# Differential attention: first block's weights split straight from its bank in all units, row sums at a unit's end, add and store in the next unit

## The chip, the core and the metric

The kernel runs on one core of a Trainium2 chip. The time is that of one execution on the device in microseconds (us). Five engines work side by side, each through its own instructions in order: PE (TensorE, matmuls and transposes; its weight loads are listed as PEld), DVE (VectorE), ACT (ScalarE), POOL (GpSimd) and SP (SyncE, which here issues the transfers). They meet only through semaphores.

## The reference

Two layers work on 1024 latent tokens and 256 context tokens of width 1024. Layer 0 has differential attention, layer 1 a state-space mixer; an MLP follows each. Only the attention of layer 0 matters here. For each of 8 heads there are two score maps, and their difference weights the values:

```python
s = jnp.einsum('bqhcd,bkhcd->bhcqk', q, k).astype(jnp.float32)
p = jax.nn.softmax(s, axis=-1)
w = p[:, :, 0] - lam * p[:, :, 1]
o = jnp.einsum('bhqk,bkhe->bqhe', w.astype(v.dtype), v)
return rmsnorm(o, subln_g) * (1.0 - lambda_init)
```

Queries and keys are rotated before (`apply_rope`), with a swap of the two halves of each head's coordinates.

## The kernel before

Everything is float32. A matmul operand is split into a high part (a copy rounded to fp32r) and a low part (the rest), and each product is three matmuls, `mm3` (lines 132 to 134): high by high, high by low, low by high.

The attention, `phase_b`, goes through 8 heads of 9 units; this text calls them head 0 to 7 and unit 0 to 8. Unit 0 takes the 256 context queries against 256 context keys, units 1 to 8 take 128 latent queries each against all 1280 keys. The order of the instructions on PE, DVE, ACT and POOL is the order in which the loop over `n` writes them (`manual_schedule`), so an instruction that waits holds up all that is written behind it on its engine.

A unit's own work is a chain: PE computes the scores (L579). DVE takes the row maximum and copies the scores out, once for each of the two maps (L592; in unit 0 L588). ACT exponentiates each (L602; in unit 0 L599), called exp 0 and exp 1 here. DVE combines the two maps into the weights: a reciprocal, a small product (L610, L611), and the long L613 over 1280 columns. In the next unit PE transposes these weights in three parts of 4, 2 and 4 tiles (L625; L620 where the unit before was unit 0), part 0, 1 and 2. Each part is split into halves in `wT` in one of two ways:

- `w_direct`: ACT copies the high half straight from PSUM (L631), DVE subtracts to get the low half (L632, it reads PSUM too);
- `w_copy`: ACT copies the part from PSUM to SBUF (L638), and POOL makes both halves from the copy (L641, L642). POOL cannot read PSUM.

One unit later, for a pair of units, PE multiplies the values (`values`, 30 `mm3` matmuls of 256 columns), ACT copies the output (L732), POOL squares it (L733), and PE sums the squares over the partitions (`pair_sums`: two L739 matmuls of one column, which write columns 0 and 1 of bank 6, then ACT's L740).

The PE also computes the next head's keys and queries in pieces called fills (`proj_group`, 8 products of three matmuls, in bank 7), in units 0, 1, 2, 3, 5 and 7; `FILLS` says how many products stand in each of the three places of a unit. In units 0, 3, 5 and 7 such a group then needs four steps: `evac` at the unit's end (ACT L528, DVE L529, and four transfers that swap halves), and three more that wait in the list `post`: `sine` (POOL L534, which waits for the swap), `add` (DVE L537), `store` (the split, ACT L137 and DVE L138). In units 1 and 2 the group has no rotation and is split at once (`direct`: L523, L524). In head 7 the fills are the output projection instead, with one product left for the last place of units 3, 5 and 7, and `out` (L855).

There are two kinds of unit. Units 4, 6 and 8 of heads 0 to 6 (`inside`) have no fills; PE does scores, half of the values, part 0 (in bank 7), the rest of the values, parts 1 and 2. Unit 1, and in head 7 units 4, 6 and 8 as well, stand in the same branch (line 946) but with fills. Units 0, 2, 3, 5 and 7 stand in the other branch (line 978): scores, part 0, a fill, parts 2 and 1, a fill. L772 (DVE) scales the outputs of the head before, in units 7, 8, 0, 1 and 2.

`next_post` runs one step of `post`. Before, the first branch calls it twice, the second once, so that `sine` and `add` come in the unit after the group and `store` in the one after that.

Of the kernel before, what the change touches and what calls it, by code (L numbers as in the profile page):

```python
# [70 lines left out]
class Prog:  # L71
# [610 lines left out]
    def phase_b(self):  # L682
# [38 lines left out]
        def values(h, pair, k0=0, k1=10):  # L721
            V = loaded[h, "v"]
            last = 2 if pair == 0 else 10
            for kt in range(k0, min(k1, last)):
                self.mm3(pb[:, 0:256], V[0][:, kt], V[1][:, kt], self.wT[0][:, kt], self.wT[1][:, kt],
                         kt == 0, kt == last - 1)
# [42 lines left out]
        def norm_pair(h, pair):  # L769
            i = nloaded.pop(0)  # L770
            (nob, nrb), (nhi, nlo) = nbufs[i], nsplit[i]
            nc.vector.scalar_tensor_tensor(nob, nob, self.sg, nrb, ALU.mult, ALU.mult)  # L772

            def halves():
                self.split(nhi, nlo, nob, nc.gpsimd)
                for j, t in enumerate((nhi, nlo)):
                    self.dma(self.on[h, j, :, 256 * pair : 256 * pair + 256], t.bitcast(F32))

            return halves
# [91 lines left out]
        def next_post():  # L871
            f = post.pop(0) if post else None
            if f:
                f()

        with self.manual():
            for n in range(72 + 5):
# [32 lines left out]
                inside = late and not groups  # L910
                low, high, last, whole = pb[:, 0:512], pb[:, 256:512], self.bank(7), self.PS[:, 1280:1792]

                def fill(i):
                    for f in fills[i]:
                        f()

                def part(i, tb):
                    return self.w_part(prev[1], prev[2], i, tb) if i < parts else None

                def direct(w):  # L920
                    if w:
                        self.w_direct(*w)

                def copied(*ws):
                    for f in [self.w_copy(*w) for w in ws if w]:
                        f()

                def exps(c):
                    if front:
                        self.exps(u, c, p, sm, s0, sn)  # L930

                def output(*a):
                    pair_out(*a)
                    sums.append((n + (parts != 1), lambda: pair_sums(*a)))
                    if a[0] == 7:
                        tail.append((n + 1, a[1]))

                def do_sums():
                    while sums and sums[0][0] <= n:
                        sums.pop(0)[1]()  # L940

                def norm():
                    if front and n - 7 >= 9 and (n - 7) % 9 < 5 and (n - 7) // 9 < 7:
                        return norm_pair((n - 7) // 9 - 1, (n - 7) % 9)

                if late or parts == 1:
                    if n == 73:
                        fill(0)
                    if inside:
                        values(*pv, 0, 5)  # L950
                        w0 = part(0, last)
                        values(*pv, 5)
                        w1, w2 = part(1, high), part(2, whole)
                    else:
                        if pv:
                            values(*pv)
                        w0, w1 = part(0, whole), part(1, high)
                    exps(0)
                    next_post()
                    exps(1)  # L960
                    if pv:
                        output(*pv)
                    next_post()
                    split = norm()
                    if front:
                        self.combine(u, p, s0, sn)
                    direct(w0)
                    if inside:
                        copied(w2, w1)
                    else:  # L970
                        copied(w1)
                        if n != 73:
                            fill(0)
                        fill(1)
                        copied(part(2, whole))
                        fill(2)
                        do_sums()
                else:
                    if pv:
                        values(*pv)  # L980
                        output(*pv)
                    fill(0)
                    w0 = part(0, low)
                    if pv:
                        exps(0)
                    direct(w0)
                    next_post()
                    if not pv:
                        exps(0)
                    exps(1)  # L990
                    fill(1)
                    w2 = part(2, whole)
                    w1 = part(1, last[:, 256:512] if pv and h < 7 else self.bank(0)[:, 0:256] if n == 72 else high)
                    copied(w2, w1)
                    do_sums()
                    if front:
                        self.combine(u, p, s0, sn)
                    fill(2)
                    split = norm()
                if groups:  # L1000
                    rest = groups[0][1]
# [1635 lines left out]
```

## Time and profile before

| what | us |
| --- | --- |
| three runs: median (lowest, highest) | 2899.28 (2891.78, 2901.7) |
| the profiled execution's own time | 2897.7 |
| its span | 2895.7 |
| attention, from head 0 unit 1 to the start of head 7 | 226.77 to 804.96 |
| head 7, units 0 to 7 | 804.96 to 884.80 |
| PE busy over the span | 2725.5 (94%) |
| DVE, ACT, POOL busy over the span | 1996.3, 1377.0, 1030.7 |
| mean granted TensorE clock | 0.986 |

A unit runs from the start of its first score matmul to that of the next unit. Times in rows are from the span's start. A number in square brackets behind a row is how long the engine stood idle before it, in us, and what ended that. A busy share that is an average over the program says little here: what counts is where PE stands still inside a unit.

### The profile page before, as it was taken

What the parts mean: (1) busy time and instruction counts of PE and PEld (TensorE: products, weight loads), DVE (VectorE), ACT (ScalarE), POOL (GpSimd) and SP (SyncE); (2) the same over time, 40 slices, a digit from 0 to 9 for tenths busy, and PEclk for the clock granted to TensorE, in tenths of its full rate; (3) what the DMA queues carried; (4) which work ended last, traced back from release to release, by engine and by line L of the source; (5) the groups of instructions that cost most, each with busy time, mean ns of one, the idle gap of its engine ahead of it and who ended that gap; (6) DMA issues with size and microseconds to landing.
All of it is one profiled execution on the core that took longest, in us unless ns stands there. A gap on an engine that the chain in (4) does not pass through costs nothing. (4 is left out here: it accounts for less than half of the span.)

```text
span 2895.7 us, 43780 instructions
## 1 busy us (share of the span) xinstructions
PE 2725.5 (94%) x15645; PEld 2261.2 (78%) x15645; DVE 1996.3 (69%) x2984; ACT 1377.0 (48%) x2584; POOL 1030.7 (36%) x902
## 2 busy tenths in 40 slices
PE   6998988999898999999999999889999999999999
PEld 4787777777777788877878788788888778888887
DVE  6366767777774467666698878799633597768566
ACT  3424555555553664333354445477543633344443
POOL 3313656666564610000030004488320243336314
PEclk9999999999999999999999999999999999999999
DMA  9953132222433448887599888569842144467544
GB/s 272 321 174 120 52 92 84 73 70 88 150 119 116 163 135 281 291 309 269 178 331 322 280 241 283 166 204 293 286 137 95 63 163 165 153 221 248 161 134 142
DMA packets 377447, 539.12 MB, mean 186 GB/s; under 512 B 38286, under 2 KB 231052, under 8 KB 374028
## 3 DMA queue, kind: packets, MB, share of 16 engines
q1 hardware_dynamic: 377228, 536.32, 57.0%
q8 instruction: 123, 2.02, 0.3%
q14 instruction: 96, 0.79, 0.1%
HBM read 367.54 MB, written 164.47 MB: 184 GB/s over the span
## 5 line engine op out<-in xcount | busy, mean ns | idle before, releaser
L132 PE MATMUL PS<-H 128*128 128x512 f32 x1072 | 420.5, 393 | 3.0 <-ACT H L137 1.9
L134 PE MATMUL PS<-H 128*128 128x512 f32 x1072 | 417.5, 390 | 2.8 <-DVE H L138 1.5
L133 PE MATMUL PS<-H 128*128 128x512 f32 x1072 | 417.7, 390 | 0.0
L132 PE MATMUL PS<-H,R 128*128 128x512 f32 (+1 forms) x828 | 308.1, 374 | 24.2 <-DVE R L632 17.7
L133 PE MATMUL PS<-H,R 128*128 128x512 f32 (+1 forms) x828 | 300.5, 363 | 0.0
L134 PE MATMUL PS<-H,R 128*128 128x512 f32 (+1 forms) x828 | 299.6, 362 | 0.0
L132 PEld LDWEIGHTS PS<-H 128*128 128x128 f32 x1072 | 201.2, 188 | 50.7 <-issue 6.2
L134 PEld LDWEIGHTS PS<-H 128*128 128x128 f32 x1072 | 201.2, 188 | 46.2 <-DVE H L138 2.4
L133 PEld LDWEIGHTS PS<-H 128*128 128x128 f32 x1072 | 201.3, 188 | 40.6
L602 ACT ACTIVATE F<-F,stat 128x1280 f32<-128x1280 f32 x128 | 174.8, 1366 | 91.2 <-DVE F L592 89.6
L132 PE MATMUL PS<-R,H 128*128 128x512 f32 x534 | 213.1, 400 | 4.0 <-ACT H L137 3.3
L137 ACT ACTIVATE H<-U 128x640 fp32r<-128x640 f32 x216 | 132.1, 674 | 173.9 <-PE PS L133 146.5
L137 ACT ACTIVATE R<-W 128x512 fp32r<-128x512 f32 (+1 forms) x185 | 129.6, 708 | 175.4 <-PE PS L133 98.9
L134 PE MATMUL PS<-R,H 128*128 128x512 f32 x534 | 210.8, 396 | 1.8 <-DVE H L138 1.8
L133 PE MATMUL PS<-R,H 128*128 128x512 f32 x534 | 209.7, 393 | 0.0
L592 DVE TENSOR_SCALAR_CACHE_REDUCE F<-PS 128x1280 f32<-128x1280 f32 x128 | 185.3, 1484 | 33.6 <-PE PS L579 32.4
L132 PEld LDWEIGHTS PS<-H,R 128*128 128x128 f32 x828 | 159.0, 192 | 55.2 <-DVE R L632 18.9
L138 DVE TENSOR_TENSOR H<-U,H 128x640 fp32r<-128x640 f32 x216 | 165.1, 798 | 52.4 <-ACT H L137 51.0
L138 DVE TENSOR_TENSOR H<-W,H 128x512 fp32r<-128x512 f32 (+1 forms) x137 | 127.4, 940 | 103.3 <-ACT H L137 103.0
L137 ACT ACTIVATE H<-W 128x512 fp32r<-128x512 f32 (+2 forms) x158 | 95.3, 613 | 186.6 <-PE PS L133 116.8
L134 PEld LDWEIGHTS PS<-H,R 128*128 128x128 f32 x828 | 158.5, 191 | 25.2 <-issue 0.8
L133 PEld LDWEIGHTS PS<-H,R 128*128 128x128 f32 x828 | 158.8, 192 | 20.9
(528 smaller groups left out, 6717.0 us busy)
## 6 DMA issues: line engine op xcount, KB each, us to landing
W<-in_mlp_w SPq DMA_DIRECT2D x176, 256.0 KB, 3.4
U<-Aa SPq DMA_DIRECT2D x108, 320.0 KB, 4.4
Aa<-FU SPq DMA_DIRECT2D x91, 320.0 KB, 4.3
Ad<-F SPq DMA_DIRECT2D x112, 256.0 KB, 2.9
W<-Ad SPq DMA_DIRECT2D x112, 256.0 KB, 2.7
FU<-in_mlp_w SPq DMA_DIRECT2D x32, 512.0 KB, 6.9
Ta<-FU SPq DMA_DIRECT2D x16, 1024.0 KB
U<-in_ada_w SPq DMA_DIRECT2D x32, 512.0 KB, 8.8
```

The costliest lines, as they stand in the source:

```text
L132: mm(out, ah, bh, start=first, stop=False, **kw)
L133: mm(out, ah, bl, start=False, stop=False, **kw)
L134: mm(out, al, bh, start=False, stop=last, **kw)
L137: self.nc.scalar.activation(hi, src, AF.Copy)
L138: (lo_eng or self.nc.vector).tensor_tensor(lo, src, hi.bitcast(F32), ALU.subtract)
L592: ts(p[c], self.PS[:, 1792 * c : 1792 * c + 1280], 1.0, None, ALU.mult, ALU.min, accum_out=sm[:, c : c + 1])
L602: nc.scalar.activation(p[c], p[c], AF.Exp, bias=sm[:, c : c + 1], scale=-1.0, accum_out=sn[:, 0:1] if c else s0[:, u + 1 : u + 2])
```

## The change

In the first branch, `inside` units split part 0 (`direct(w0)`) right behind exp 0 instead of behind the combine, and only one step of `post` runs. In the second branch, part 1 is split by `w_direct` instead of `w_copy`, behind the combine; a second step of `post` runs behind that; and the row sums (`do_sums`, L739 and L740) move behind the last fill. So `sine` stays in the unit after its group, and `add` and `store` both come one unit later, `add` ahead of the combine and `store` behind it.

```diff
                     exps(0)
+                    if inside:
+                        direct(w0)
                     next_post()
                     exps(1)
                     if pv:
                         output(*pv)
-                    next_post()
                     split = norm()
                     if front:
                         self.combine(u, p, s0, sn)
-                    direct(w0)
                     if inside:
                         copied(w2, w1)
                     else:
+                        direct(w0)
                         copied(w1)
...
                     w2 = part(2, whole)
                     w1 = part(1, last[:, 256:512] if pv and h < 7 else self.bank(0)[:, 0:256] if n == 72 else high)
-                    copied(w2, w1)
-                    do_sums()
+                    copied(w2)
                     if front:
                         self.combine(u, p, s0, sn)
+                    direct(w1)
+                    next_post()
                     fill(2)
+                    do_sums()
                     split = norm()
```

The counts change for 40 units: 40 L638 copies of 256 columns become L631 copies, 40 L632 of 256 columns are added on DVE, and 40 L641 and 40 L642 of 256 columns leave POOL. PE, SP and the work outside the attention keep their instructions; only their order changes, and only within the attention and the few instructions behind it. Line numbers of the changed kernel behind line 958 are higher by up to 3.

The first place is DVE from unit 8 into the next head's unit 0. R_110 holds `wT` (and the halves of weights), F_1851 the scores and weights of the units, FC the rotation's buffers. Before:

```order
L592 TENSOR_SCALAR F_1851,stat<-PS 128x1280 x2
L537 TENSOR_TENSOR FC<-FC 128x512
L772 SCALAR_TENSOR_TENSOR W<-W,lamc 128x256
L610 RECIPROCAL stat<-stat 128x1
L611 SCALAR_TENSOR_TENSOR stat<-FC,stat,lamc 128x1
L613 SCALAR_TENSOR_TENSOR F_1851<-F_1851,stat 128x1280
L632 TENSOR_TENSOR R_110<-PS,R_110 128x4x128
L588 TENSOR_SCALAR F_1851,stat<-PS 128x256 x4
```

And with the change:

```order
L592 TENSOR_SCALAR F_1851,stat<-PS 128x1280 x2
L632 TENSOR_TENSOR R_110<-PS,R_110 128x4x128
L772 SCALAR_TENSOR_TENSOR W<-W,lamc 128x256
L610 RECIPROCAL stat<-stat 128x1
L611 SCALAR_TENSOR_TENSOR stat<-FC,stat,lamc 128x1
L613 SCALAR_TENSOR_TENSOR F_1851<-F_1851,stat 128x1280
L588 TENSOR_SCALAR F_1851,stat<-PS 128x256 x4
L632 TENSOR_TENSOR R_110<-PS,R_110 128x4x128
L537 TENSOR_TENSOR FC<-FC 128x512
```

Part 0's L632 has moved ahead of the combine, and the add (L537) from ahead of unit 8's combine to unit 0, behind that unit's maxima and its own L632.

The second place is PE at the end of unit 5, where the row sums stand. The names in brackets are the semaphores that the instruction waits for, one for each engine. Before, from the end of the transposes of parts 2 and 1:

```order
L625 MATMUL PS<-ident,F_1851 128x128 [waits DVE_49]
L625 MATMUL PS<-ident,F_1851 128x128
L739 MATMUL PS<-lamc,adat 128x1 [waits Activation_49]
L739 MATMUL PS<-lamc,adat 128x1
L132 MATMUL PS<-H,R_110 128x512
```

And with the change, from the last matmul of the last fill:

```order
L134 MATMUL PS<-H,R_110 128x512
L739 MATMUL PS<-lamc,adat 128x1 [waits DVE_49,Pool_49]
L739 MATMUL PS<-lamc,adat 128x1
L758 MATMUL PS<-ident,FC 10x128 [waits Activation_49,Pool_49]
L579 MATMUL PS<-R_1850 128x512 x12
```

The sums now stand behind nine fill matmuls and directly ahead of the next unit's scores (L758 is there in unit 5 alone), and they wait for DVE where they waited for ACT: for the L632 of part 1, which reads the same bank.

The third place is DVE from unit 2 into unit 3. Before:

```order
L632 TENSOR_TENSOR R_110<-PS,R_110 128x4x128
L138 TENSOR_TENSOR R_1850<-FC,R_1850 128x512
L610 RECIPROCAL stat<-stat 128x1
L611 SCALAR_TENSOR_TENSOR stat<-FC,stat,lamc 128x1
L613 SCALAR_TENSOR_TENSOR F_1851<-F_1851,stat 128x1280
L772 SCALAR_TENSOR_TENSOR W<-W,lamc 128x256
L524 SCALAR_TENSOR_TENSOR R_110<-PS,R_1850 128x256
L592 TENSOR_SCALAR F_1851,stat<-PS 128x1280 x2
```

And with the change:

```order
L632 TENSOR_TENSOR R_110<-PS,R_110 128x4x128
L537 TENSOR_TENSOR FC<-FC 128x512
L610 RECIPROCAL stat<-stat 128x1
L611 SCALAR_TENSOR_TENSOR stat<-FC,stat,lamc 128x1
L613 SCALAR_TENSOR_TENSOR F_1851<-F_1851,stat 128x1280
L632 TENSOR_TENSOR R_110<-PS,R_110 128x2x128
L138 TENSOR_TENSOR R_1850<-FC,R_1850 128x512
L772 SCALAR_TENSOR_TENSOR W<-W,lamc 128x256
L524 SCALAR_TENSOR_TENSOR R_110<-PS,R_1850 128x256
L592 TENSOR_SCALAR F_1851,stat<-PS 128x1280 x2
```

Between the combine and L524 there are now two more DVE instructions, part 1's L632 and the store's L138; the add has the place that the store had.

## The prediction

> **What bounds the kernel now.** I read first the busy time by stretches: each row has its start and end, its length, the busy time of PE, PEld, DVE, ACT and POOL, then the granted clock and the share and rate of the transfers.
>
> ```profile
> 226.77:804.96 578.19, 515.91 (x3634) 438.58 (x3634) 418.60 (x676) 325.64 (x638) 345.42 (x337) 0.98 0.29 90
> 804.96:884.80 79.84, 71.93 (x460) 59.64 (x459) 56.98 (x94) 43.93 (x88) 46.49 (x50) 0.96 0.30 92
> ```
>
> PE is busy for 516 of 578 us in the attention before head 7; DVE, next, has 419. So PE sets the pace, and the 62 us in which it stands still (more where its clock is low) are what a new order can win. Next, who ended PE's waits in the attention (total us, times, longest):
>
> ```profile
> PE PS L739 <- ACT F L638: 25.5, 31, 1.6
> PE PS L132 <- DVE R L632: 17.7, 6, 5.3
> PE PS L625 <- DVE F L613: 13.0, 21, 2.8
> PE PS L579 <- DVE R L632: 6.3, 2, 5.5
> ```
>
> These four hold nearly all of it: the row sums wait for the copies out of PSUM; fills and scores wait for part 0's low half; transposes wait for the combine. Then single units: unit 0 of heads 1 to 6; unit 2 of heads 0 and 5; unit 5 of heads 0, 5, 6; unit 7 of heads 1, 5.
>
> ```profile
> 304.15:315.49 11.34, 8.51 (x52) 6.67 (x52) 7.62 (x20) 5.44 (x17) 7.50 (x9) 1.00 0.03 12
> 385.44:401.72 16.28, 10.22 (x52) 8.00 (x51) 9.90 (x23) 5.85 (x18) 9.49 (x11) 0.79 0.30 87
> 471.89:486.98 15.09, 10.10 (x51) 7.88 (x51) 9.75 (x23) 5.85 (x18) 8.71 (x10) 0.89 0.31 87
> 557.68:569.13 11.45, 8.50 (x52) 6.70 (x52) 9.45 (x23) 5.74 (x18) 8.46 (x10) 1.00 0.30 93
> 638.77:650.11 11.34, 8.52 (x51) 6.68 (x50) 9.33 (x22) 5.72 (x18) 8.19 (x10) 1.00 0.30 93
> 719.82:732.79 12.97, 10.08 (x52) 7.90 (x52) 7.64 (x22) 5.73 (x18) 8.28 (x10) 0.87 0.29 91
> 236.46:251.24 14.78, 9.25 (x60) 8.25 (x60) 8.98 (x14) 5.20 (x10) 3.10 (x3) 0.77 0.18 57
> 659.50:666.34 6.84, 6.84 (x61) 6.26 (x60) 5.09 (x8) 4.92 (x10) 2.60 (x3) 1.00 0.75 246
> 268.20:279.82 11.62, 9.58 (x57) 7.51 (x57) 9.55 (x14) 6.33 (x13) 7.95 (x7) 1.00 0.07 23
> 684.70:695.47 10.77, 9.71 (x58) 7.60 (x57) 8.61 (x12) 6.34 (x13) 9.39 (x8) 1.00 0.03 12
> 767.38:780.66 13.28, 9.68 (x58) 7.59 (x57) 12.77 (x14) 7.27 (x14) 12.58 (x11) 1.00 0.49 168
> 366.98:378.63 11.65, 9.61 (x57) 7.47 (x56) 10.31 (x15) 6.86 (x14) 9.26 (x8) 1.00 0.10 31
> 702.32:712.99 10.67, 9.61 (x57) 7.46 (x56) 9.59 (x13) 6.85 (x14) 8.59 (x8) 1.00 0.07 24
> ```
>
> The same unit with the same instructions takes 11.34 or 16.28, 6.84 or 14.78. The long ones have a reason to be looked for in the timeline; some also ran at a granted clock of 0.77 to 0.89, behind their long wait.
>
> **Unit 8 into unit 0 (part 0 early, add out of the way).** Head 4 into head 5, the ordinary case:
>
> ```profile
> 636.94 1.37 ACT L602 ACTIVATE F<-F,stat 128x1280 f32<-128x1280 f32 x1
> 639.56 1.55 DVE L613 SCALAR_TENSOR_TENSOR F<-F,stat 128x1280 f32<-128x1280 f32 x1
> 641.03 0.68 DVE L632 TENSOR_TENSOR R<-PS,R 128x512 fp32r<-128x512 f32 x1
> 641.77 0.50 PE L132 MATMUL PS<-H,R 128*128 128x512 f32 x1 [2.02 <-DVE R L632]
> 642.57 0.60 PE L625 MATMUL PS<-ident,F 128*128 128x128 f32 x4
> 647.41 0.61 PE L739 MATMUL PS<-lamc,adat 128*128 128x1 f32 x4 [0.80 <-ACT F L638]
> ```
>
> Unit 0's first fill writes bank 7, which unit 8's part 0 still occupies until its L632, and that stands behind the add and the combine. With the change L632 is done before the combine, so the 2.02 go. What is late next is the combine itself, for the transposes 0.80 further on. Part 0's ACT copy (L631) now comes between exp 0 and exp 1 and takes 0.6, 0.5 of it net of the overlap of two neighbours, so exp 1 starts at 637.45 and ends at about 639.0. The add is gone, so DVE scales (L772) before that, and L613 starts 0.48 behind exp 1, at 639.5, as now. Its end: 641.05 at the 1.55 of the row, 641.45 where POOL's square (L733), which now falls in the same moment as in units 4 and 6, stretches it to 1.9 (the 1.88 quoted with the rivals). I take 641.45: the transposes go from 642.57 to 641.5, a gain of 1.07 (bounds 1.45 and 0). With the 0.80 of the row sums, whose L739 goes behind nine fill matmuls (about 2.2 us of cover), a unit 0 of 11.34 becomes 9.47.
>
> The long ones: in head 2 the swap's transfers came late.
>
> ```profile
> 385.05 1.28 POOL L534 TENSOR_TENSOR FC<-FC,W 128x512 f32<-128x512 f32 x1 [3.00 <-DMA FC<-FC]
> 386.36 1.08 DVE L537 TENSOR_TENSOR FC<-FC 128x512 f32<-128x512 f32 x1 [2.78 <-POOL FC L534]
> ```
>
> DVE stood at the add for 2.78 us with the combine and L632 behind it, and PE for 5.26. With the change the add stands in the next unit, behind unit 0's maxima and its L632, some 4 us later than the 386.33 at which this sine ended; it waits for nothing. So I set all six to 9.47: 11.34 + 16.28 + 15.09 + 11.45 + 11.34 + 12.97 = 78.47, less 6 x 9.47 = 56.82, is **21.7**. For the same reason unit 2 of head 0, where scores waited 5.5 for unit 1's part 0 behind a late add, goes from 14.78 to 6.84, the same unit without a wait: **7.9**. Units 5 of heads 0 and 6 and unit 7 of head 1, whose transposes waited for a combine behind a late add, go to the ordinary 10.77 and 10.67: 0.85 + 2.51 + 0.98 = **4.3**.
>
> **Units 4 to 8, ordinary.** What pays for this is exp 1, 0.5 later in units 4 and 6. Unit 5 of head 5:
>
> ```profile
> 686.94 0.63 PE L625 MATMUL PS<-ident,F 128*128 128x128 f32 x4 [0.24 <-DVE F L613]
> 692.19 1.55 DVE L613 SCALAR_TENSOR_TENSOR F<-F,stat 128x1280 f32<-128x1280 f32 x1
> 692.63 0.61 PE L739 MATMUL PS<-lamc,adat 128*128 128x1 f32 x4 [0.82 <-ACT F L638]
> 693.28 0.17 ACT L740 ACTIVATE FC<-PS 128x2 f32<-128x2 f32 x1 [0.70 <-PE PS L739]
> ```
>
> The combine of unit 4 already ends last for these transposes, so they start 0.4 later. Then the 0.82 goes, since the fill follows at once, and L739 comes at 692.63 + 0.4 - 0.82 + 2.26 (nine matmuls) = 694.5. There it waits for part 1's L632, behind the combine: L613 ends at 693.74, or 0.2 earlier because unit 4's L632 no longer stands ahead of unit 5's maxima; a 256-column L632 adds 0.34 (the 0.41 of L524 below, net of overlap), so 693.9 to 694.1. It is covered by 0.4. In unit 5 alone L758 follows, and it waits for L740: 0.8 behind L739's start instead of the usual 0.5, which costs 0.35. Per head: unit 5 gains 0.82 - 0.4 - 0.35, nearly nothing; unit 7 gains 0.82 - 0.4 = 0.4.
>
> **Units 2 and 3.** Unit 2 into 3 of head 5:
>
> ```profile
> 664.92 0.62 ACT L137 ACTIVATE R<-FC 128x512 fp32r<-128x512 f32 x1
> 665.66 0.68 DVE L138 TENSOR_TENSOR R<-FC,R 128x512 fp32r<-128x512 f32 x1
> 667.37 1.55 DVE L613 SCALAR_TENSOR_TENSOR F<-F,stat 128x1280 f32<-128x1280 f32 x1
> 669.60 0.41 DVE L524 SCALAR_TENSOR_TENSOR R<-PS,R 128x256 fp32r<-128x256 f32 x1
> 670.06 0.50 PE L132 MATMUL PS<-H,R 128*128 128x512 f32 x1 [0.43 <-DVE R L524]
> ```
>
> The store's ACT copy (664.92) leaves the place between exp 0 and exp 1, so the combine is 0.52 earlier. Behind it come L632 (0.34) and the store's L138 (0.60) ahead of L524, and PE's fill waits for L524: 0.42 later. Unit 3 then loses 0.42, saves 0.74 at its row sums, and finds part 1's L632 about 0.1 late: a gain of 0.25. Of that unit 5 takes most back, because unit 4's maxima start hardly earlier: they stand behind the evac's L529, which now waits for L740 too. I count 0.4 per head, what unit 7 gains (bounds 0.65, all three added, and nil), times 7: **2.9**.
>
> By the Trainium skill, "PSUM — Partial Sum Buffer", section "PSUM bank collisions raise a hardware error", PSUM is to be guarded by bank, not by address. The trace agrees: L739 writes columns 0 and 1 and waited 0.82 for a copy of columns 256 to 511. So the rule speaks against this change, as the sums now wait for a later instruction on the same bank; guarded by address they would not, and the loss below would be nil, and the sum 2862.
>
> **Head 7.** Its units 3, 5 and 7 have three matmuls as cover, unit 0 none.
>
> ```profile
> 841.28 1.55 DVE L613 SCALAR_TENSOR_TENSOR F<-F,stat 128x1280 f32<-128x1280 f32 x1
> 841.67 0.61 PE L739 MATMUL PS<-lamc,adat 128*128 128x1 f32 x4 [0.74 <-ACT F L638]
> ```
>
> L613 ends at 842.83, L632 at 843.17. The scores, now 0.47 + 0.88 behind 841.67 at 843.02, start 0.47 behind 843.17: 0.6 later. Units 5 and 7, where the norm's matmul also follows L740, lose about 1.0 each, unit 0 about 0.5. Some is taken up where DVE is late anyway: **-2.5**.
>
> The rest of the change hides: POOL loses 80 instructions, but no PE wait names it; 40 L632 of 0.34 are on DVE behind the combines counted above.
>
> **The sum.** 21.7 + 7.9 + 4.3 + 2.9 - 2.5 = 34.3. From the profiled execution's 2897.7: 2863.4. It stands 1.6 under the median, so I predict **2865** for the median.
>
> **The rivals.**
>
> 1. *Late adds still block* (2890). The add is again ahead of a combine. If swaps come late by more than a unit, the long units stay long: 7.9 + 4.3 + 21.7 - 6 x 1.87 = 22.7 of the gain is lost, 2888, and noise on top. Against it: the latest sine seen in a unit 0 ended 0.9 into it. 6%.
> 2. *The combine is as late as L632 was* (2871). L613 takes the freed time, the 1.07 in each of six units 0 is nil. For it: it is the next wait at once. 17%.
> 3. *The sums wait for the combine in every head* (2879 to 2910). Cover is 0.4 in unit 5 and none in unit 3. This execution has combines of
>
> ```profile
> 368.18 1.88 DVE L613 SCALAR_TENSOR_TENSOR F<-F,stat 128x1280 f32<-128x1280 f32 x1
> ...
> 473.74 2.65 DVE L613 SCALAR_TENSOR_TENSOR F<-F,stat 128x1280 f32<-128x1280 f32 x1
> ```
>
> while POOL worked: up to 1.1 over the 1.55. In each of 27 units 0, 3, 5, 7 that would cost some 0.5 to 0.9 above its cover, 14 to 24: 2879 to 2889, 8%. It becomes slower than before from 34.3 + 8.7 = 43 over 27 units, 1.6 above cover, 2.0 of delay each: 2908 or more, 3%. By the Trainium skill, "SBUF — State Buffer", section "Who interferes with whom", a DVE instruction with two SBUF inputs and a POOL instruction lock each other out, and the first to start goes on; the trace agrees with the 2.65. POOL's copies start just behind L613 in units 3, 5 and 7, so by that rule it is POOL that waits.
> 4. *The change does nothing* (2890 to 2908): each wait is replaced by another of its size. 5%.
>
> **The numbers.** Forecast (2857 to 2871 without rival 2) 55%, rival 2 17%, rival 1 6%, rival 3 8% and 3%, no change 5%, and 6% for more than I count: two units 2 of heads 2 and 3 that were also near 1 us long, combines of 1.55, no loss in head 7, a clock that no longer falls; 2852 or less. So the range is 2852 to 2886. A run tells a change from none at about 0.3%, 8.7 us: under 2890.6 is faster. Faster: forecast, rivals 2 and 3 in its first part, the case of more, and half of rival 1, 55 + 17 + 8 + 6 + 3 = 89%. Within: the other half and most of rival 4, 7%. Slower: rival 3 in its second part and the rest of rival 4, 4%.
>
> **What would show it.** Right: no wait of L132 or L579 for L632 over 1 us, all units 0 of heads 1 to 6 within 9 to 10 us, a mean clock there of 1.00; L739 waiting under 0.2 in units 0, 5 and 7, and in head 7 for DVE's L632 by 1 us or more; L625 of unit 5 waiting some 0.6 for L613. Wrong: L739 waits of 0.5 or more for L632 in heads 0 to 6, or an L537 with idle time ahead of it in units 2, 5, 7 and 0.

## The result

| | before | after |
| --- | --- | --- |
| median of 4 runs each, us | 2898.31 (2891.78 to 2901.7) | 2872.57 (2865.49 to 2876.93) |
| ratio, 95% interval | | 0.9912 (0.9884 to 0.9939) |
| span of the profiled execution, us | 2895.7 | 2868.5 |
| attention, from the first unit to the start of head 7's unit 8, us | 664.9 | 639.9 |

The change makes the kernel 25.7 us faster. Forecast were 34.3 us and a median of 2865; the time lies inside the range, 7.6 above the forecast and 1.6 above the narrower 2857 to 2871 that the prediction held for most likely.

The sum by its terms, from the lengths of the units in the two profiled executions (a unit runs from its first score matmul to that of the next):

| term | forecast gain, us | measured gain, us |
| --- | --- | --- |
| units 0 of heads 1 to 6: 78.5 to 57.2 | 21.7 | 21.3 |
| unit 2 of head 0: 14.78 to 6.81 | 7.9 | 8.0 |
| late adds: unit 5 of heads 0 and 6, unit 7 of head 1 | 4.3 | 6.4 |
| the other units 3, 5 and 7 of heads 0 to 6 | 2.9 | -0.4 |
| head 7: 79.85 to 89.83 | -2.5 | -10.0 |
| all other units | 0 | -0.3 |
| sum | 34.3 | 25.0 |

Two terms failed: head 7, and units 3. What ended PE's waits in the attention now (total us, times, longest):

```profile
PE PS L625 <- DVE F L613: 16.3, 21, 2.3
PE PS L132 <- DVE R L524: 11.6, 7, 2.1
PE PS L739 <- POOL R L641: 8.4, 14, 1.7
PE PS L739 <- DVE R L632: 6.1, 1, 6.1
```

The waits of L132 and L579 for L632, 17.7 and 6.3 before, are gone. In their place stand a wait for L524 in each unit 3 (five of 2.0 to 2.1 us, two of 0.7) and one of 6.1 in unit 0 of head 7. Before, the waits for L524 were small:

```profile
PE PS L132 <- DVE R L524: 2.1, 5, 0.4
```

The third row of the list above names L641, but that one is not the releaser. In unit 7 of head 5

```profile
681.47 1.80 POOL L641 TENSOR_SCALAR R<-F 128x512 fp32r<-128x512 f32 x1 [1.15 <-ACT F L638]
682.70 0.42 DVE L632 TENSOR_TENSOR R<-PS,R 128x256 fp32r<-128x256 f32 x1
683.27 0.35 PE L739 MATMUL PS<-lamc,adat 128*128 128x1 f32 x2 [0.31 <-POOL R L641]
```

L641 ends in the moment in which L739 starts, and L632 ended 0.15 before it, the same step as from L632's end (782.10) to L739's start (782.25) in unit 0 of head 7 below, where L641 had ended 2.1 earlier. The step is 0.15 in all 15 of these waits, so the sums wait for L632, as was foreseen for head 7.

**Units 3.** Unit 2 into 3 of head 4, DVE, POOL and PE:

```profile
558.62 1.55 DVE L613 SCALAR_TENSOR_TENSOR F<-F,stat 128x1280 f32<-128x1280 f32 x1
560.09 0.42 DVE L632 TENSOR_TENSOR R<-PS,R 128x256 fp32r<-128x256 f32 x1
560.42 0.76 DVE L138 TENSOR_TENSOR R<-FC,R 128x512 fp32r<-128x512 f32 x1
561.11 1.48 DVE L772 SCALAR_TENSOR_TENSOR W<-W,lamc 128x256 f32<-128x256 f32 x1
562.51 0.41 DVE L524 SCALAR_TENSOR_TENSOR R<-PS,R 128x256 fp32r<-128x256 f32 x1
...
560.74 1.57 POOL L642 TENSOR_TENSOR R<-F,R 128x512 fp32r<-128x512 f32 x1
...
562.98 0.80 PE L132 MATMUL PS<-H,R 128*128 128x512 f32 x1 [2.10 <-DVE R L524]
563.58 0.63 PE L133 MATMUL PS<-H,R 128*128 128x512 f32 x1
564.00 0.63 PE L134 MATMUL PS<-H,R 128*128 128x512 f32 x1
```

L632 and L138 came ahead of L524 as foreseen. But L772 now starts 0.37 after POOL's L642 instead of ahead of it, and takes 1.48 instead of 0.83. Even the 0.83 held a wait: L772 then ended 0.27 behind the end of POOL's L641 (head 5), as it ends 0.28 behind that of L642 here. From the end of L613 to the start of L524 it is 2.34 us; before it was 0.68 (head 5). PE waits 2.10. Then its matmuls L133 and L134 start 0.42 apart, where behind the same wait in head 5 it is 0.23:

```profile
642.43 0.50 PE L132 MATMUL PS<-H,R 128*128 128x512 f32 x1 [2.10 <-DVE R L524]
642.76 0.39 PE L133 MATMUL PS<-H,R 128*128 128x512 f32 x1
642.99 0.40 PE L134 MATMUL PS<-H,R 128*128 128x512 f32 x1
```

The difference is the granted clock. Units 3 of heads 3, 4, 5, then stretches of 3.41 us behind the waits in heads 2, 3, 4 and 5 (start and end, length, busy time of PE, PEld, DVE, ACT and POOL, clock, transfers):

```profile
478.45:491.33 12.88, 10.91 (x57) 8.79 (x56) 10.26 (x15) 6.31 (x12) 5.74 (x5) 0.87 0.10 32
558.11:571.19 13.08, 10.88 (x58) 8.71 (x57) 10.47 (x17) 6.34 (x13) 6.00 (x5) 0.87 0.10 31
637.70:649.71 12.01, 9.59 (x59) 7.51 (x58) 10.29 (x16) 6.23 (x12) 6.48 (x5) 1.00 0.10 34
...
402.39:405.80 3.41, 3.41 (x9) 2.62 (x9) 3.12 (x5) 2.57 (x4) 0.63 (x1) 0.50 0.36 115
484.31:487.72 3.41, 3.41 (x10) 2.64 (x9) 2.46 (x7) 2.86 (x4) 0.00 (x0) 0.50 0.26 78
562.82:566.23 3.41, 3.25 (x8) 2.58 (x9) 3.41 (x6) 2.57 (x5) 0.73 (x1) 0.50 0.37 115
642.37:645.78 3.41, 3.35 (x15) 2.78 (x16) 3.41 (x6) 2.58 (x5) 0.74 (x1) 1.00 0.35 115
```

For exactly 3.41 us PE runs at half its clock and gets 8 to 10 matmuls done instead of 15. That is worth about 0.9 us of a unit 3: head 4's takes 13.08, head 6's, with the same wait and a clock of 1.00, 12.16.

**Unit 0 of head 7**: DVE's two combines of 256 columns, L632 and PE's sums behind them:

```profile
777.13 2.54 DVE L613 SCALAR_TENSOR_TENSOR F<-F,stat 128x256 f32<-128x256 f32 x1
...
780.18 1.58 DVE L613 SCALAR_TENSOR_TENSOR F<-F,stat 128x256 f32<-128x256 f32 x1
781.69 0.41 DVE L632 TENSOR_TENSOR R<-PS,R 128x256 fp32r<-128x256 f32 x1
...
782.25 0.98 PE L739 MATMUL PS<-lamc,adat 128*128 128x1 f32 x4 [6.14 <-DVE R L632]
```

The first L613 takes 2.54 where the other heads' of this size take 0.48 to 0.94: POOL's split of output weights (L138, 128x1024, 2.34 us) had started 0.09 ahead of it, and it ended 0.29 behind that. Before the change it took 2.54 as well, but the sums waited only for ACT's copy, and the scores ran while the second L613 was at work. With no fill in that unit nothing of 6.14 is covered, and the clock stands at 0.50 for 13.65 us:

```profile
774.44:788.09 13.65, 6.53 (x30) 5.36 (x31) 9.76 (x13) 3.94 (x14) 7.62 (x8) 0.50 0.43 137
```

### The profile page after: what moved, and what is told of

The parts are those of the page before. It is cut to its first block, busy times and chain, and to the rows that moved or that the text cites. A ratio compares the mean times of both kernels' runs of the same rounds, so it can differ in the third digit from the quotient of the medians.

```text
span 2868.5 us, 43793 instructions
## 1 busy us (share of the span) xinstructions
PE 2721.0 (95%) x15645; PEld 2263.1 (79%) x15645; DVE 2026.8 (71%) x3024; ACT 1373.3 (48%) x2584; POOL 983.5 (34%) x822
## 5 line engine op out<-in xcount | busy, mean ns | idle before, releaser
L132 PE MATMUL PS<-H 128*128 128x512 f32 x1072 | 420.5, 393 | 2.3 <-ACT H L137 1.5
L134 PE MATMUL PS<-H 128*128 128x512 f32 x1072 | 417.5, 390 | 3.0 <-DVE H L138 1.7
L133 PE MATMUL PS<-H 128*128 128x512 f32 x1072 | 417.7, 390 | 0.0
L132 PE MATMUL PS<-H,R 128*128 128x512 f32 (+1 forms) x828 | 307.9, 374 | 15.8 <-DVE R L524 11.6
L133 PE MATMUL PS<-H,R 128*128 128x512 f32 (+1 forms) x828 | 300.4, 363 | 0.0
L134 PE MATMUL PS<-H,R 128*128 128x512 f32 (+1 forms) x828 | 299.9, 363 | 0.0
L132 PEld LDWEIGHTS PS<-H 128*128 128x128 f32 x1072 | 201.1, 188 | 50.3 <-issue 6.2
L134 PEld LDWEIGHTS PS<-H 128*128 128x128 f32 x1072 | 201.2, 188 | 46.1 <-DVE H L138 2.6
L133 PEld LDWEIGHTS PS<-H 128*128 128x128 f32 x1072 | 201.3, 188 | 40.5
L132 PE MATMUL PS<-R,H 128*128 128x512 f32 x534 | 212.7, 399 | 3.9 <-ACT H L137 3.2
L134 PE MATMUL PS<-R,H 128*128 128x512 f32 x534 | 210.7, 396 | 1.7 <-DVE H L138 1.7
L133 PE MATMUL PS<-R,H 128*128 128x512 f32 x534 | 209.6, 393 | 0.0
L138 DVE TENSOR_TENSOR H<-U,H 128x640 fp32r<-128x640 f32 x216 | 165.6, 800 | 55.0 <-ACT H L137 54.9
L138 DVE TENSOR_TENSOR H<-W,H 128x512 fp32r<-128x512 f32 (+1 forms) x137 | 127.1, 939 | 103.2 <-ACT H L137 102.8
L132 PEld LDWEIGHTS PS<-H,R 128*128 128x128 f32 x828 | 158.6, 192 | 45.4 <-DVE R L524 13.3
L134 PEld LDWEIGHTS PS<-H,R 128*128 128x128 f32 x828 | 158.5, 191 | 25.6 <-issue 0.8
L133 PEld LDWEIGHTS PS<-H,R 128*128 128x128 f32 x828 | 158.9, 192 | 21.1
```

The costliest lines, as they stand in the source:

```text
L132: mm(out, ah, bh, start=first, stop=False, **kw)
L133: mm(out, ah, bl, start=False, stop=False, **kw)
L134: mm(out, al, bh, start=False, stop=last, **kw)
L138: (lo_eng or self.nc.vector).tensor_tensor(lo, src, hi.bitcast(F32), ALU.subtract)
```

## The experiments

Each is one kernel with its own profile; times are given as a ratio to the kernel before on the same chip, and where parts of the attention are compared, from the profiles. The attention's length is that of the first table, from one execution of each kernel. What lies outside the attention took 2219.9 to 2231.3 us in these 14 executions, and that is part of each ratio too; so differences of a few us count only where rows show their cause. The first three kernels make one part of the change alone, on the kernel before.

**Part 0 early, alone** (in units 4, 6, 8).

```diff
                     exps(0)
+                    if inside:
+                        direct(w0)
                     next_post()
...
-                    direct(w0)
                     if inside:
                         copied(w2, w1)
                     else:
+                        direct(w0)
```

> The kernel before with one part of the change: in units 4, 6 and 8 part 0 is split between exp 0 and exp 1; add, store, part 1 and row sums stay where they were. My theory (the parts only pay together, since the combine still stands behind the add): the fills' wait for L632 goes, the transposes wait for L613 instead; an ordinary unit 0 loses 0.9 to 1.4 of its 11.34 us, the three long ones (16.28, 15.09, 12.97) stay over 12.5, unit 2 of head 0 stays near 14.8, and units 5 and 7 lose about 0.3 each by the later exp 1: 2893 to 2897. Rival (the place of part 0 is the main thing): the whole L132 wait of 17.7 goes with little in its place, units 0 all under 10.3, 2884 or less.

Measured: 0.9983 (0.9969 to 0.9997), attention 656.7, 8.2 less. The fills' wait is gone, and the transposes wait for the combine instead (25.6 us for L613 against 13.0 before). Ordinary units 0 are 10.1 to 10.6, those of heads 2 and 3 are still 13.9 and 13.8 long, and unit 2 of head 0 is 14.6. Head 6's unit 0 is 10.66, shorter than I had it, and ordinary units 5 and 7 lose 0.1 each where I had 0.3. The theory holds in the main.

**Add and store later, alone.**

```diff
                         output(*pv)
-                    next_post()
                     split = norm()
...
                         self.combine(u, p, s0, sn)
+                    next_post()
                     fill(2)
```

> The kernel before with one part of the change: add and store run in the next unit that has a group; part 0, part 1 and the row sums stay. My theory (the loss of 5.4 us in units 3 of heads 1 to 6 comes from the store and the scaling that now stand ahead of L524): units 3 of heads 2 to 6 are longer than before by 0.5 to 1.5 with L132 waiting 1.2 or more for L524; the late adds no longer hold anything, so unit 2 of head 0 is 6.9, units 5 are 10.8, and units 0 of heads 1 to 6 are all about 11.0: 2881 to 2886. Rival (the loss in units 3 comes from part 1's L632 and the moved sums): units 3 as before, 11.5, and 2875 to 2878.

Measured: 0.9972 (0.9958 to 0.9987), which is 8.1 us, but in the profiled execution's attention only 1.3 less. Units 3 of heads 2 to 6 are 12.7 to 14.3 instead of 11.3 to 11.6, with the wait for L524 at 2.10, though there is no L632 of part 1 in this kernel. So the loss in units 3 is that of the moved store: L138 stands there ahead of L772, which takes 1.48 in each of them. Where I was wrong is units 0: not 11.0 but 12.7 to 13.0, except in head 6. Here are unit 0 of heads 5 and 6, then unit 3 of the same heads:

```profile
633.68:646.33 12.65, 10.08 (x51) 7.95 (x51) 8.30 (x21) 5.73 (x18) 7.95 (x10) 0.87 0.32 92
718.71:729.80 11.09, 8.52 (x51) 6.68 (x50) 8.50 (x21) 5.74 (x18) 7.96 (x10) 1.00 0.39 105
662.55:676.82 14.27, 11.33 (x58) 8.61 (x58) 10.05 (x15) 6.40 (x14) 8.28 (x9) 0.88 0.09 30
746.03:758.73 12.70, 9.75 (x58) 7.47 (x57) 10.05 (x15) 6.32 (x14) 8.39 (x7) 1.00 0.44 136
```

The waits are the same in both heads, 1.77 in unit 0 and 2.10 in unit 3; a lowered clock makes each unit of head 5 1.6 longer. Eleven such stretches stand in this attention, six in the kernel before.

**Part 1 straight from its bank and sums at the end, alone.**

```diff
-                    copied(w2, w1)
-                    do_sums()
+                    copied(w2)
                     if front:
                         self.combine(u, p, s0, sn)
+                    direct(w1)
                     fill(2)
+                    do_sums()
```

> The kernel before with one part of the change: part 1 is split straight from its bank behind the combine, and the row sums stand at the unit's end; add, store and part 0 stay. My theory: the L739 wait of 0.8 goes in heads 0 to 6, an ordinary unit 0 is 10.5, unit 5 10.3, unit 7 10.1, unit 3 11.2 or less with its L524 wait 0.4 longer; head 7 loses 3 to 5 in units 3 to 7 because its sums wait 1.5 each for L632: 2886 to 2890 (the long units stay long). Rival (this part is what costs in units 3): units 3 of heads 2 to 6 are 12 to 13, and the total 2893 to 2897.

Measured: 1.0013 (1.0 to 1.0027), attention 5.0 longer. Units 3 and the ordinary units 0 gain as expected (10.2 to 11.1, and 10.3 to 10.4), so the rival's mechanism is out, though its total is the nearer one. Units 7 are 9.6 to 10.6. Units 5 do not gain: they are 10.7 to 11.0 where I had 10.3, and 13.1 and 13.9 in heads 0 and 6. Head 7 is 88.8, 8.9 more where I had 3 to 5, and the units 0 of heads 2 and 4 are 15.3 and 15.1 long: in these the add stood waiting 2.1 and 1.5 for its sine, with the combine and the L632 behind it, and the fills waited 4.6 and 4.2 for that L632. The add's wait is not all of it: ahead of head 5's unit 0 the add waited 1.2, and the fill only 2.2. There L613 started 0.21 ahead of POOL's L641 and took 1.55; ahead of head 4's it started within 0.05 us of POOL's L642 and took 2.65. In units 3, L772 here follows L632 at once, ahead of L642, in head 4:

```profile
584.39 0.42 DVE L632 TENSOR_TENSOR R<-PS,R 128x256 fp32r<-128x256 f32 x1
584.73 0.50 DVE L772 SCALAR_TENSOR_TENSOR W<-W,lamc 128x256 f32<-128x256 f32 x1
585.26 0.42 DVE L524 SCALAR_TENSOR_TENSOR R<-PS,R 128x256 fp32r<-128x256 f32 x1
...
585.04 1.32 POOL L642 TENSOR_TENSOR R<-F,R 128x512 fp32r<-128x512 f32 x1
```

0.50 for L772 where it starts 0.31 ahead of L642, against 1.48 where it starts 0.37 behind it.

The next three take one part out of the whole change.

**Without part 0 early.** Edit: the first diff above, undone in the changed kernel.

> The changed kernel without the early split of part 0 in units 4, 6 and 8; add and store, part 1 and row sums as in the change. My theory (each part removes a wait that would otherwise come next, so each is worth more in company than alone): alone this part took 8 us off the attention; left out of the whole it costs 9 to 14, most of it in units 0, whose fills wait about 2 again. Rival (the parts are independent): it costs 8 or less.

Measured: 0.9933 (0.9918 to 0.9948), attention 645.8. The part costs 6.0 us of attention when left out, and alone it gained 8.2; the ratio cannot be told apart from that of the whole change. The fills of units 0 wait for L632 again, 0.9 to 2.7 each. The rival holds: this part is worth about the same alone and in company.

**Without add and store later.** Edit: the second diff, undone in the changed kernel.

> The changed kernel with add and store where they were before (one call between the exps and one behind the values' output in units 1, 4, 6, 8, one call in the others). Alone this part took 1 us off the attention, gaining 14 in units 0, 5 and in head 0 and losing 12 in units 3. My theory: left out of the whole, units 0 get their late adds back (66 to 70 us in heads 1 to 6 against 57), head 0 loses 7 or more, and units 3 come down to 65 to 67 from 73.8: 6 to 14 us longer than the change. Rival (the loss in units 3 outweighs it now that L632 of part 0 is early): the same time or less than the change.

Measured: 0.9958 (0.9944 to 0.9971), attention 660.7, 20.9 longer than with the whole change, where I had 6 to 14. Head 0 loses 10.5, and units 3 come down to 66.1, both as expected. Units 0 of heads 1 to 6 lose only 5.4 together: they are 62.6 where I had 66 to 70. I had missed units 5: heads 5 and 6 have 14.6 and 13.6. In head 5 the add waited 1.46 for its sine ahead of unit 4's combine, and the transposes 3.3 for that; in head 6 the sums waited 2.0 for L632.

**Without the sums and part 1.** Edit: the third diff, undone in the changed kernel, with the store still behind the combine.

> The changed kernel with part 1 copied and the row sums ahead of the combine, as before the change; part 0, add and store as in the change. Alone the moved sums with part 1's split cost 5 us, 9 of it in head 7. My theory: left out of the whole, L739 waits 0.8 for L638 again in heads 0 to 6, units 5 and 7 are 0.4 to 0.6 longer each, units 0 about 0.8 longer, units 3 as long as with add and store moved alone (80), head 7 is 80 to 81: 5 to 12 us longer than the change. Rival (the sums bring nothing net): within 3 us of the change.

Measured: 0.9948 (0.9934 to 0.9963), attention 649.0, 9.2 longer. L739 waits 25.4 us for L638, as before the change, unit 5 is 10.85, units 0 are 61.5 together, units 3 are 79.4, head 7 is 80.0: all as expected.

In attention time the three parts alone give 8.2, 1.3 and -5.0, 4.5 together; the whole gives 25.0. In the ratios the parts give 0.0032 together and the whole 0.0088. The last two need each other: alone they give -3.7 together, and in one kernel, without part 0 early, 19.1. Sums behind the combine are only good where no late add holds the combine. Another share is the clock. With one part each, the attention ran at half clock for 23.9, 41.0 and 58.0 us, before the change for 30.7, and with all of it for 30.7 again. So the three parts alone add 30.8 us of half clock in all, nine steps of 3.41 us, and the whole adds none. At 0.9 to 1.6 us for a step (the last section) that is an estimated 8 to 14 of the 20.5 us that the whole gives beyond its parts.

**Part 1 by copy again, sums still at the end.**

```diff
-                    copied(w2)
+                    copied(w2, w1)
                     if front:
                         self.combine(u, p, s0, sn)
-                    direct(w1)
                     next_post()
                     fill(2)
                     do_sums()
```

> The changed kernel with part 1 of units 0, 2, 3, 5, 7 again copied by ACT (L638) and split by POOL, the rest of the change kept, the row sums at the unit's end. My theory (the sums are served by their place; the split straight from the bank makes them wait for the combine and is what costs head 7): head 7's L739 waits for L632 go, and it returns to 80 to 83 us from 89.8; units 0, 5, 7 of heads 1 to 6 keep their length within 0.2; units 3 are 0.3 shorter: 2860 to 2866. Rival (POOL's ten additional instructions a head hold the port or POOL itself, so that combines and L632s come later): units 5 and 7 of heads 1 to 6 lose 0.5 or more each, 2873 to 2880.

Measured: 0.9870 (0.9847 to 0.9893), attention 627.2, 12.6 less than with the change. Head 7 is 80.3, as expected. Units 7 of heads 1 to 6 are not the same but 0.53 shorter each:

```profile
673.65:683.77 10.12, 9.31 (x57) 7.49 (x56) 9.90 (x15) 6.43 (x13) 8.33 (x8) 1.00 0.07 22
...
670.37:679.98 9.61, 9.10 (x57) 7.57 (x56) 9.38 (x13) 6.47 (x13) 7.88 (x7) 1.00 0.05 18
```

(head 5, the change and this kernel). 0.31 of it is the sums' wait for L632. Units 3 stay: L524 still waits for the store and L772, 2.0 to 2.1 in heads 2 to 6, and four of those ran with a lowered clock. So the split of part 1 straight from its bank costs about 12 us, 9.5 of them in head 7; the gain is in the place of the sums, part 0 and the add.

**Head 7 as before** (part 1 by copy, sums ahead of the combine), the rest as in the change.

```diff
-                    copied(w2)
+                    if h < 7:
+                        copied(w2)
+                    else:
+                        copied(w2, w1)
+                        do_sums()
                     if front:
                         self.combine(u, p, s0, sn)
-                    direct(w1)
+                    if h < 7:
+                        direct(w1)
...
                     fill(2)
-                    do_sums()
+                    if h < 7:
+                        do_sums()
```

> The changed kernel, but in head 7 part 1 is copied and the row sums stand ahead of the combine, as in the kernel before; part 0, add and store as in the change. My theory: L739's waits for L632 of 6.1, 1.6, 1.7 and 1.7 go, those for ACT of 0.7 to 1.6 come back; units 3 to 7 return to 50.5 and unit 0 to 8 to 10 us, so head 7 is 79.5 to 82 instead of 89.8: 2863 to 2865. Rival (head 7's loss comes from transfers that are late and not from the sums): units 0 stays over 12, and the total at 2868 to 2871.

Measured: 0.9865 (0.9850 to 0.9879). Head 7 is 81.85, its unit 0 9.22, with the sums' wait at

```profile
777.16 1.01 PE L739 MATMUL PS<-lamc,adat 128*128 128x1 f32 x4 [1.30 <-ACT F L638]
```

The theory holds: the sums' place behind L632 is the loss.

**Scaling ahead of the combine in unit 7 of head 6.**

```diff
                     copied(w2)
+                    if n == 61:
+                        split = norm()
                     if front:
...
                     do_sums()
-                    split = norm()
+                    if n != 61:
+                        split = norm()
```

> The changed kernel, but in unit 7 of head 6 alone the scaling (L772) stands ahead of the combine. It is the instruction that SP's queue waits for there, 2.4 us later than in the kernel before, with the swap's transfers and the output's behind it. My theory (this makes the swap late, so that sine, add and part 0's L632 in unit 0 of head 7 are late): the first of SP's issues behind it comes 2 us earlier, the waits of unit 0 of head 7 for L632 fall by 2 to 4 in all, its length from 13.9 to 10 to 12: 2 to 4 us less. Rival (only the order of sums and combines counts there): unit 0 of head 7 stays within 0.7 of 13.9.

Measured: 0.9892 (0.9876 to 0.9909), unit 0 of head 7 13.34 instead of 13.91, the sums still waiting

```profile
783.83 0.98 PE L739 MATMUL PS<-lamc,adat 128*128 128x1 f32 x4 [5.63 <-DVE R L632]
```

My theory finds no support. The first issue behind L772 came 4.4 us earlier, but the swap's first transfer only 0.7, since it then waited 2.6 for ACT's L528, and the output weights that ACT waits for there (2.40, before the edit 2.46) did not come earlier at all. Late transfers were thus hardly tested; the run before this one shows that head 7 gets its time back without them.

**Store behind L524 in unit 2.**

```diff
                     direct(w1)
-                    next_post()
+                    if u != 2:
+                        next_post()
...
                     rest[0]()
+                    if u == 2:
+                        next_post()
```

> The changed kernel, but in unit 2 the store stands behind the group's own split (L523, L524) and not ahead of it. My theory: the L132 wait for L524 in units 3 of heads 2 to 6, 2.0 to 2.1 us now, falls to 0.4 to 0.9 (L772 and part 1's L632 are left ahead), units 3 are 11.4 to 11.8 instead of 12.0 to 13.1: 5 to 7 us less, 2865 to 2868. Rival (POOL's halves of part 2 stretch whatever DVE does behind the combine): L772 or L524 takes the stretch, the wait stays over 1.5, and the time within 2 us of the changed kernel's.

Measured: 0.9895 (0.9878 to 0.9912). The mechanism is as expected: in head 4

```profile
562.00 0.49 DVE L772 SCALAR_TENSOR_TENSOR W<-W,lamc 128x256 f32<-128x256 f32 x1
562.53 0.42 DVE L524 SCALAR_TENSOR_TENSOR R<-PS,R 128x256 fp32r<-128x256 f32 x1
563.04 1.14 DVE L138 TENSOR_TENSOR R<-FC,R 128x512 fp32r<-128x512 f32 x1
...
562.31 1.33 POOL L642 TENSOR_TENSOR R<-F,R 128x512 fp32r<-128x512 f32 x1
...
563.01 0.50 PE L132 MATMUL PS<-H,R 128*128 128x512 f32 x1 [0.55 <-DVE R L524]
```

PE waits 0.55 instead of 2.10, all units 3 have a clock of 1.00, and in heads 1 to 6 they take 69.0 instead of 73.8. But the stretch falls on the store, which holds unit 3's own chain: part 1's L632 comes later, and the sums now wait 0.8 for it. Of the 4.7 us gained there 3.5 are lost again in one unit 2 (head 2), where transposes waited 2.8 for ACT's L732. The cause of that one is open. The time is not told apart from that of the change.

**Both of these edits.**

> The changed kernel with both: in unit 2 the store behind L524, and head 7's part 1 and row sums as in the kernel before. If the two losses are separate, as I think, their gains add: 12 to 16 us below the changed kernel, 2856 to 2860. Rival (one only moves the wait to another place): 8 us or less below it, 2864 or more.

Measured: 0.9858 (0.9841 to 0.9875), attention 628.3, 11.6 less than with the change; the two edits alone had 1.3 and 7.7. In the ratio it is 0.0054, 15.6 us. So neither takes from the other, and the rival is out.

**A version from all of this**: part 1 by copy, sums at the end, and in unit 2 both the store and the scaling behind L524.

```diff
-                    copied(w2)
+                    copied(w2, w1)
...
-                    direct(w1)
-                    next_post()
+                    if u != 2:
+                        next_post()
                     fill(2)
                     do_sums()
-                    split = norm()
+                    if u != 2:
+                        split = norm()
...
                     rest[0]()
+                    if u == 2:
+                        next_post()
+                        split = norm()
```

> The changed kernel with part 1 copied (L638) and split by POOL, sums still at the unit's end, and in unit 2 the store and the scaling behind the group's own split (L524). My theory (in units 3 L524 is held by store and scaling, of which L772 takes 1.48 us where POOL's L642 has started before it, and PE's 2.0 us of standing still is what lowers its clock to 0.87 there): units 3 of heads 1 to 6 wait under 0.4 for L524, run at a clock of 1.00 and take 9.8 to 10.5 instead of 13.1: 10 to 13 us less than with part 1 copied alone, 0.982 to 0.984 of the kernel before. Rival (store and scaling, put behind L524, hold unit 3's maxima or its part 0 instead): units 3 of 11 or more, 0.986.

Measured: 2847.61 us, 0.9843 (0.9828 to 0.9857), attention 615.5: 49.4 less than before, 24.4 less than with the change. Units 3 of heads 2 and 4, and in head 4 L524 and the L132 behind it:

```profile
398.05:408.55 10.50, 9.48 (x58) 7.54 (x57) 9.47 (x13) 6.08 (x12) 6.67 (x6) 1.00 0.12 40
552.94:563.72 10.78, 9.55 (x58) 7.48 (x57) 9.67 (x15) 6.11 (x13) 6.91 (x6) 1.00 0.12 39
...
554.92 0.42 DVE L524 SCALAR_TENSOR_TENSOR R<-PS,R 128x256 fp32r<-128x256 f32 x1
...
555.47 0.48 PE L132 MATMUL PS<-H,R 128*128 128x512 f32 x1
```

No wait is left ahead of L132. Part 0 of unit 3 now waits 0.8 to 1.0 for the maxima behind the store and the scaling, so the rival has its share: units 3 are 10.5 to 10.8, not 9.8. The clock is lowered twice in this attention, in unit 1 of head 0 and in unit 0 of head 7.

## Why the prediction was right and where it failed

- **Units 0, the late adds, unit 2 of head 0**: right, 35.7 measured for 33.9. The part that is taken furthest from rows, the combine as the next wait, came out: units 0 are 9.53 on average for 9.47, without a wait for L632, at a clock of 1.00. One was 8.91 and one 10.09, so the bound of 9 to 10 was a little narrow. No L537 stands waiting in the attention now, and the three long ones have come down to the others.
- **Unit 5 and unit 7**: unit 7 gains 0.5 (0.4 forecast), ordinary units 5 0.5 too (nearly nothing forecast). Their transposes wait 0.5 for L613 instead of the 0.64 that I had.
- **"PE's fill waits for L524: 0.42 later" in "Units 2 and 3" failed.** L632, L138 and an earlier combine were counted rightly; L772 was taken with its old 0.83, and it took 1.48 once it stood behind the store. L524 comes 0.8 to 1.2 later in heads 2 to 6. And the forecast had no term for what a longer wait does to the clock. Together units 3 of heads 1 to 6 lost 5.4 where 1.5 were to be gained.
- **"unit 0 about 0.5" in "Head 7" failed**: it lost 5.8. The rows for the right number stood in the profile before:

```profile
814.68 1.60 DVE L613 SCALAR_TENSOR_TENSOR F<-F,stat 128x256 f32<-128x256 f32 x1
...
812.12 1.01 PE L739 MATMUL PS<-lamc,adat 128*128 128x1 f32 x4 [1.61 <-ACT F L638]
```

  There the sums ran at 812.12, and the second L613 ended at 816.28. A sum that waits for an L632 behind that must come 4 us later. The prediction has rows of unit 3 of head 7 alone and gives its 0.5 without a row of unit 0, which has two L613, late and slow behind POOL's instructions. Units 3, 5 and 7 lost 0.7, 1.3 and 1.4 for 0.6, 1.0 and 1.0; unit 6 lost 1.5, in a stretch of lowered clock.
- **The rivals**: rivals 1 and 4 did not come. Rival 2, a combine as late as L632 was, holds in part for head 2 (the transposes waited 1.72, the unit took 10.09) and hardly for the others (waits of 0.6 to 1.4, units of 8.9 to 9.7). Rival 3, sums that wait for the combine, came with 0.3 to 0.4 in units 7 and in units 3 of heads 0, 1, 5 and 6, and in full in head 7. The sign of being right, under 0.2 in units 7, was thus missed, and the sign of being wrong, 0.5 or more, did not show.
- The port: by the Trainium skill, "SBUF — State Buffer", section "Who interferes with whom", the instruction that is first to take the shared port goes on and the other one waits. The prediction concluded that in units 3, 5 and 7 it is POOL that would wait for L613. It did: the combines of these units took 1.55 or 1.56 in every head. What the prediction left out is the next instructions: L772 took 0.50 when it started ahead of L642 and 1.48 when it started behind, so the runs agree with the rule there too.

That the total came within 7.6 us is in part luck: losses of 7.5 us in head 7 and 3.3 in units 3, 5 and 7 were not foreseen, and neither were gains of 2.1 more from the late adds and of 2.2 from outside the attention (the span is 27.2 shorter, the attention 25.0). The 2.2 lie within what that rest varies by from one execution to the next.

## What to carry to other kernels

Work that is moved behind another instruction gets that instruction's worst case, so look up the latest end of it in every kind of unit, the odd one (here unit 0 of the last head) first. What an instruction costs beside one of another engine can depend on which of the two starts first, so a row's duration holds only for the order in which it was measured. And where PE stands still for about 2 us, count the clock too: two changes that each leave such a wait can be worth little alone and much together.

## What was not expected of the hardware

The granted clock follows a fixed grid. In the changed kernel the lowered stretches quoted above begin at 402.39, 484.31 and 562.82, which is 24 and 23 times 3.413 us apart; all those of one execution fit one such grid. A stretch is 0.50 of full speed and lasts one step of it, or several. Over the attention of the 14 kernels profiled here, with PE's idle time added up in each step that ran at full clock:

| PE idle in a step of 3.41 us | steps | followed by half clock |
| --- | --- | --- |
| under 1.5 us | 2411 | 3 |
| 1.5 to 1.82 us | 27 | 9 |
| over 1.82 us | 70 | 70 |

So a wait of 2.1 us costs another 0.9 to 1.6 if it lies in one step, as in head 4 (560.88 to 562.98, with steps from 559.41 and 562.82), and nothing if it lies across two, as in head 5 (640.33 to 642.43, with a step from 641.33). Where the grid lies is another matter in each execution.

The Trainium skill, "TensorE: Matmul & The Clock Gate", section "Part 1: The HAM clock gate (the "warmup" mystery)", has this window: 3413 ns, free-running, with half and full clock as the two states of this gate. The runs agree. It puts the return to half clock behind an idle window of about 3.4 us; here the measurement differs, since a little over half a window of idle time was enough.
